# Forming sums of weight blocks once and keeping them in DRAM, in a gated encoder layer on one core

## The chip, the cores and the metric

The kernel runs on one core of one Trainium2 chip. The metric is the device time of one execution in microseconds, and the kernel's time is the median over runs. Every run of a kernel computes the same layer for two sequences of 1024 tokens, the "prompt" and the "sample".

## The reference, cut to what matters

The layer is a gated mix of three token mixers, an output projection with a residual and a layer norm, a SwiGLU feed-forward block, and a second residual and layer norm. All of it is float32. The part that this change touches is the products with `w_gate`, `w_up` and `w_down`:

```python
m = (g[..., :D_MODEL] * ya + g[..., D_MODEL:2 * D_MODEL] * yb + g[..., 2 * D_MODEL:] * yc)
x = layer_norm(DEEPNORM_ALPHA * x + (m @ w_out).astype(x.dtype), ln1_g, ln1_b)
f = (jax.nn.silu(x @ w_gate) * (x @ w_up)) @ w_down        # 1024 -> 2816 -> 1024
x = layer_norm(DEEPNORM_ALPHA * x + f.astype(x.dtype), ln2_g, ln2_b)
```

The same weights serve both sequences.

## The kernel before, in words

**Split products.** Every float32 operand is split into a high half (`wh`, a cast on ScalarE, line 159) and a low half (`wl`, a subtraction on VectorE, line 160), both 128x512 "pages" in a pool of 94 pages. `mm3` (lines 108 to 110) makes one product from three matmuls: high by high, high by low, low by high. A page is 256 KB.

**Quartets.** The products with gate, up and down follow a seven-product scheme for two by two blocks (Strassen's, in Winograd's form). A quartet is four weight blocks B11, B21, B12, B22, each one page. Its seven products use B11, B21, B22 and four sums of blocks: numbers 5 (B12-B11), 6 (B22 minus number 5), 7 (B22-B12) and 4 (B21 minus number 6). `quartet_units` (line 134) lists which raw blocks each product needs; `prepare` (line 162) makes the four sums on GpSimd (line 173, tiles `wt`), 7 us of planned time ahead of the split (`PREP`), and for the first four quartets of a sequence 14 us earlier still (`early`); `split_unit` (line 187) splits whichever page the product needs. One sequence has 22 quartets for gate and up: 11 pairs of column blocks, indexed p = 0 to 10 (`NP` is 11), each with a gate and an up quartet. `w_down` has 11 quartets, used once for both sequences. Two times 22 and 11 make 55 quartets and 220 sums.

**Stages.** For each sequence: the input projections with neighbourhood attention, linear attention and pooling as side work; three gate branches (`gate_branch`, the last one with `w_br_a`); `wout` (16 chunks of 24 matmuls); `gate_up` (154 chunks of 12 matmuls, one product each). After both sequences comes `down`, in five parts of 2, 2, 2, 2 and 3 quartets; each part runs over four token tiles and both sequences, and each such step is seven products of 6 (or 9) matmuls. `gate_up` stores its result in DRAM as split operands, and `down` loads them again (tiles `a`, line 1387).

**Order.** A list of chunks, each with its planned length, is run in order by `run`. Before each chunk, `advance` splits the units that fall due, makes sums `PREP` ahead, and fetches raw pages up to `nraw` (7, and 4 from `down` on) beyond those that are used up. All these loads, and the stores of operands, go out from SyncE's queue, in program order, each waiting there for a free page or for the data that it stores. The `Side` queue holds small steps of other work; chunks call `side.tick`, which runs steps at the rate that `attach` set, and `side.drain` runs what is left. VectorE, ScalarE and GpSimd execute in the program's order too, so a late instruction holds up what stands behind it.

Of the kernel before, what the change touches and what calls it, by code (L numbers as in the profile page):

```python
# [8 lines left out]
F32 = mybir.dt.float32  # L9
# [3 lines left out]
ALU = mybir.AluOpType  # L13
# [64 lines left out]
class Kernel:  # L78
    def __init__(self, tc, ins, xs, ys, pools):
# [12 lines left out]
        self.nraw = NRAW  # L92

# [40 lines left out]
    def quartet_units(self, src, early=0.0):  # L134


        blocks = {}
        for k, j in ((1, 1), (2, 1), (1, 2), (2, 2)):
            ap = src(k, j)
            n, w = ap.shape[1], ap.shape[2]  # L140
            blocks[k, j] = dict(src=[(ap, 0, w)], n=n, w=w)
        q = dict(blocks=blocks, tmp={})
        use = {1: ((1, 1),), 2: ((2, 1),), 6: ((1, 1), (1, 2), (2, 2)), 5: ((1, 1), (1, 2)) if early else (),
               7: ((1, 2), (2, 2)), 4: ((2, 1),), 3: ((2, 2),)}
        return {i: dict(raws=[blocks[x] for x in use[i]], q=q, i=i, early=early if i in (4, 5, 6, 7) else 0.0) for i in use}
# [17 lines left out]
    def prepare(self, u):  # L163
# [12 lines left out]
        if i in (5, 6) and 5 not in tmp:  # L176
            comb(5, B(1, 2), B(1, 1))
        if i == 6:
            comb(6, B(2, 2), tmp[5])
# [67 lines left out]
    def advance(self, upto):  # L247
# [11 lines left out]
        while n < len(order) and order[n]["t"] - order[n].get("early", 0.0) <= upto + PREP:  # L259
            n += 1  # L260
# [758 lines left out]
    def wout(self, S, s):  # L1019
# [198 lines left out]

    def gate_up(self, S, x1_stages, at_end, end_us):
# [5 lines left out]
        for p in range(NP):  # L1225
            for n in ("w_gate", "w_up"):
                src = lambda k, j: self.w_cols(n, (2 * p + j - 1) * 128, 128, 4 * k - 4, 4)
                qs.append(dict(p=p, gate=n == "w_gate", ops=self.quartet_units(src, 14.0 if p < 2 else 0.0)))
# [121 lines left out]
    def down(self, Ss):  # L1350
# [3 lines left out]
        def row(p):  # L1354
            w = self.ins["w_down"][0]
            return lambda k, j: w[(2 * p + k - 1) * 128:(2 * p + k) * 128, (j - 1) * 512:j * 512].rearrange("p (o c) -> p o c", o=1)
# [5 lines left out]
        for part in parts:  # L1362
            ops = [self.quartet_units(row(p)) for p in part]
# [203 lines left out]
    def sequence(self, Ss, s):  # L1567
# [14 lines left out]

        hook(after_cv)
# [8 lines left out]
        def na0():  # L1592
            side.drain()
# [145 lines left out]
```

## Time and profile before

| | us |
|---|---|
| median of 3 runs | 2943.52 (2942.41 to 2944.05) |
| the profiled execution's own time | 2941.66 |
| its span in the trace | 2939.7 |
| TensorE busy | 2850.9 (97%) |
| VectorE busy | 1684.5 (57%) |
| ScalarE busy | 1031.8 (35%) |
| GpSimd busy | 694.5 (24%) |
| granted TensorE clock, mean | 0.988 |

The page gives shares over the whole span, and stages with different limits stand in it side by side. Stages are found in the trace by their tile names: `mh` are the operands of `w_out`, `x1h` those of gate and up, `a` those of down. The `w_out` stage of the first sequence ends at 801 us of the span. 345.06 MB go through the DMA queues in 1410 transfers of SyncE and a few of others.

### The profile page before, as it was taken

To read this page: it belongs to the slowest core of one execution; us is meant where nothing else is said; L and a number is where in the kernel's file an instruction comes from. 1 tells how busy PE (TensorE), PEld (TensorE's weight loads), DVE (VectorE), ACT (ScalarE), POOL (GpSimd) and SP (SyncE) were. 2 spreads that over 40 slices of the span, in tenths; PEclk is the share of its full clock that TensorE was granted. 3 is DMA by queue.
4 is the path that set the end of the run, shared out by engine and by line. 5 is a ranking of instruction groups with operands and counts; after the bars stand their busy time and mean duration, and the time that the engine had idled before them with its cause. 6 is when DMAs were issued, how large, how long until landed. Compare 5 with 4: busy or idle time off the path is not lost.

```text
span 2939.7 us, 39440 instructions
## 1 busy us (share of the span) xinstructions
PE 2850.9 (97%) x14216; PEld 2397.0 (82%) x14216; DVE 1684.5 (57%) x2936; ACT 1031.8 (35%) x2135; POOL 694.5 (24%) x819
## 2 busy tenths in 40 slices
PE   8999999999989999999999999998999999999997
PEld 7888898888767888789888988887788887877876
DVE  5453633433677776673536344347777766567576
ACT  5423322222144444454334122212444444422221
POOL 3221200000222332202202000004133332144367
PEclk9999999999999999999999999999999999999999
DMA  8111111114204655581111111143165554977775
GB/s 223 40 31 44 37 47 43 48 43 133 91 31 136 175 155 158 148 229 51 27 43 47 36 46 46 43 122 108 29 181 161 157 158 149 313 252 255 226 235 198
DMA packets 461346, 345.06 MB, mean 117 GB/s; under 512 B 28257, under 2 KB 395984, under 8 KB 461088
## 3 DMA queue, kind: packets, MB, share of 16 engines
q1 hardware_dynamic: 458800, 337.75, 38.8%
q0 software_dynamic: 2208, 4.74, 0.6%
q8 instruction: 112, 1.84, 0.3%
q14 instruction: 82, 0.67, 0.1%
q10 hardware_dynamic: 144, 0.07, 0.0%
HBM read 242.81 MB, written 102.27 MB: 117 GB/s over the span
## 4 chain that ended last, share of the span: by engine, by line
PE 86%; DVE 8%; ACT 3%; issue 2%; DMA 1%; POOL 1%; SPq 0%; POOLq 0%; DVEq 0%; ACTq 0%
PE ps_m L108 26%; PE ps_m L110 26%; PE ps_m L109 26%; DVE wl L160 3%; PE ps_s L949 1%; PE ps_s L109 1%; PE ps_s L110 1%; PE ps_s L108 1%; DVE x1l L1119 1%; PE ps_s L699 1%; PE ps_s L931 1%; PE ps_s L716 0%; PE ps_s L670 0%; PE ps_s L715 0%; DVE x1s L1132 0%
## 5 line engine op out<-in xcount | busy, mean ns | idle before, releaser
L110 PE MATMUL ps_m<-x1h,wl 128*128 128x512 f32 x1040 | 410.9, 395 | 25.9 <-DVE wl L160 25.8
L108 PE MATMUL ps_m<-xTh,wh 128*128 128x512 f32 x1088 | 435.6, 400 | 0.0
L110 PE MATMUL ps_m<-xTh,wl 128*128 128x512 f32 x1088 | 425.4, 391 | 0.0
L109 PE MATMUL ps_m<-xTl,wh 128*128 128x512 f32 x1088 | 424.8, 390 | 0.0
L108 PE MATMUL ps_m<-x1h,wh 128*128 128x512 f32 x1040 | 409.9, 394 | 3.3 <-ACT wh L159 3.3
L109 PE MATMUL ps_m<-x1l,wh 128*128 128x512 f32 x1040 | 408.9, 393 | 2.1 <-DVE x1l L1119 2.1
L160 DVE TENSOR_TENSOR wl<-raw,wh 128x512 fp32r<-128x512 f32 (+1 forms) x429 | 309.0, 755 | 141.1 <-ACT wh L159 99.5
L173 POOL TENSOR_TENSOR wt<-raw 128x512 f32<-128x512 f32 x110 | 171.2, 1564 | 555.4 <-PE ps_m L109 184.7
L110 PEld LDWEIGHTS ps_m<-x1h,wl 128*128 128x128 f32 x1040 | 197.7, 190 | 72.1 <-DVE wl L160 31.2
L108 PE MATMUL ps_m<-wh,a 128*128 128x512 f32 x616 | 242.6, 394 | 12.0 <-DVE x L1407 4.9
L159 ACT CAST wh<-raw 128x512 fp32r<-128x512 f32 (+1 forms) x429 | 240.1, 604 | 34.4 <-PE ps_m L109 19.7
L109 PE MATMUL ps_m<-wl,a 128*128 128x512 f32 x616 | 241.4, 392 | 0.0
L110 PE MATMUL ps_m<-wh,a 128*128 128x512 f32 x616 | 241.4, 392 | 0.0
L110 PEld LDWEIGHTS ps_m<-xTh,wl 128*128 128x128 f32 x1088 | 204.6, 188 | 43.7 <-DVE wl L160 0.2
L108 PEld LDWEIGHTS ps_m<-xTh,wh 128*128 128x128 f32 x1088 | 205.0, 188 | 41.6 <-issue 1.0
L109 PEld LDWEIGHTS ps_m<-xTl,wh 128*128 128x128 f32 x1088 | 204.9, 188 | 41.0 <-issue 1.0
L108 PEld LDWEIGHTS ps_m<-x1h,wh 128*128 128x128 f32 x1040 | 197.7, 190 | 45.8 <-ACT wh L159 5.2
L109 PEld LDWEIGHTS ps_m<-x1l,wh 128*128 128x128 f32 x1040 | 197.4, 190 | 44.9 <-DVE x1l L1119 4.1
L160 DVE TENSOR_TENSOR wl<-wt,wh 128x512 fp32r<-128x512 f32 x220 | 201.0, 923 | 35.7 <-ACT wh L159 31.6
L999 DVE SCALAR_TENSOR_TENSOR gt<-gt,ps_m 128x512 f32<-128x512 f32 x96 | 65.9, 686 | 270.7 <-PE ps_m L110 263.0
L1216 ACT COPY u<-ps_m 128x512 f32<-128x512 f32 x168 | 98.6, 587 | 320.1 <-PE ps_m L110 302.1
L173 POOL TENSOR_TENSOR wt<-raw,wt 128x512 f32<-128x512 f32 x110 | 170.3, 1554 | 89.0 <-DVE wl L160 27.6
(263 smaller groups left out, 5466.2 us busy)
## 6 DMA issues: line engine op xcount, KB each, us to landing
a<-a SPq DMA_DIRECT2D x264, 256.0 KB, 4.4
raw<-in_w_in SPq DMA_DIRECT2D x168, 256.0 KB, 3.2
a<-wh SPq DMA_DIRECT2D x154, 256.0 KB, 2.9
a<-wl SPq DMA_DIRECT2D x154, 256.0 KB, 3.1
raw<-in_w_gate SPq DMA_DIRECT2D x88, 256.0 KB, 3.6
raw<-in_w_up SPq DMA_DIRECT2D x88, 256.0 KB, 3.9
raw<-in_w_down SPq DMA_DIRECT2D x44, 256.0 KB, 3.8
a<-a SPq DMA_DIRECT2D x88, 128.0 KB, 4.0
```

The costliest lines, as they stand in the source:

```text
L108: mm(out, a[0], b[0], start=start, stop=False, **kw)
L109: mm(out, a[0], b[1], start=False, stop=False, **kw)
L110: mm(out, a[1], b[0], start=False, stop=stop, **kw)
L159: self.nc.scalar.copy(hi, src)
L160: self.side.after.append((of, lambda: self.nc.vector.tensor_tensor(out=lo, in0=src, in1=hi, op=ALU.subtract)))
L173: self.nc.gpsimd.tensor_tensor(out=p, in0=x, in1=y, op=ALU.subtract)
L699: nc.tensor.matmul(bb[:, sl], blk(S.k[h], j)[64:128], blk(S.q[h], j)[64:128], start=True, stop=True)
L931: nc.tensor.transpose(b[0:n, i * 128:i * 128 + 128], s[:, i * 120:i * 120 + n], self.ident)
L949: nc.tensor.matmul(o, v[0:n], p[0:n, i * 128:i * 128 + 128], start=(i == 0), stop=(i == 2))
L999: nc.vector.scalar_tensor_tensor(out=t, in0=t, scalar=1.0, in1=y, op0=ALU.add, op1=ALU.mult)
L1119: self.side.after.append((None, lambda: self.nc.vector.tensor_tensor(out=lo, in0=src, in1=hi, op=ALU.subtract)))
L1216: self.nc.scalar.copy(p, b)
```

## The change

Sums are formed once per quartet and kept in a DRAM tile (`keep`: 128 x 4 x 512, one page per sum). A quartet that is met a second time, or whose sums were made ahead, has seven units with one raw page each, which are loaded as they are and split (`one=True`); GpSimd does nothing for it. A quartet of the first sequence that was not made ahead is summed on GpSimd as before, and `split_unit` adds a store of each sum.

`sum_steps` makes sums ahead, as side steps: load four blocks, two empty steps, four subtractions in place, an empty step, four stores. Items alternate between GpSimd and VectorE. For the first sequence these are ten items: the gate and up quartets of p = 0, 1, 9 and 10, and down's first two quartets; five of them are attached ahead of the last gate branch (over 76 us of planned time) and five at the start of `wout` (over 62 us). For the second sequence they are down's other nine quartets, five and four at the same places. `early` is gone. `nraw` is 4 from the first projections of a sequence to the start of `wout`, where it goes back to 7, and 5 instead of 4 in `down`. The `side.drain()` at the head of `na0` is dropped.

```diff
+    SUMS = (5, 6, 7, 4)
+    def quartet_units(self, key, src):
+        blocks = {x: src(*x) for x in ((1, 1), (2, 1), (1, 2), (2, 2))}
+        n, w = blocks[1, 1].shape[1:]
+        raw = lambda ap: dict(src=[(ap, 0, w)], n=n, w=w)
+        if key in self.kept:
+            d = self.kept[key]
+            whole = {1: blocks[1, 1], 2: blocks[2, 1], 3: blocks[2, 2]}
+            for j, i in enumerate(self.SUMS):
+                whole[i] = d[:, j, :].rearrange("p (a b) -> p a b", a=n)
+            return {i: dict(raws=[raw(whole[i])], one=True) for i in whole}
+        d = self.keep(key)
 ...
+    def sum_steps(self, items):
+        nc = self.nc
+        steps, nop = [], lambda: None
+        for j, (key, src) in enumerate(items):
+            d, B = self.keep(key), {}
+            e = nc.vector if j % 2 else nc.gpsimd
+            def load(B=B, src=src):
+                for x in ((1, 1), (1, 2), (2, 2), (2, 1)):
+                    ap = src(*x)
+                    B[x] = self.page("tb")
+                    nc.sync.dma_start(out=B[x].rearrange("p (a b) -> p a b", a=ap.shape[1]), in_=ap)
+            def sums(out, x, y, B=B, e=e):
+                e.tensor_tensor(out=B[out], in0=B[x], in1=B[y], op=ALU.subtract)
+            def store(B=B, d=d):
+                for j, x in enumerate(((1, 1), (2, 2), (1, 2), (2, 1))):
+                    nc.sync.dma_start(out=d[:, j, :], in_=B.pop(x))
+            steps += [load, nop, nop, lambda f=sums: f((1, 1), (1, 2), (1, 1)), lambda f=sums: f((1, 2), (2, 2), (1, 2)),
+                      lambda f=sums: f((2, 2), (2, 2), (1, 1)), lambda f=sums: f((2, 1), (2, 1), (2, 2)), nop, store]
+        return steps
 ...
     def split_unit(self, u):
             src = q["tmp"][u["i"]]
+            if u["i"] in self.SUMS:
+                self.nc.sync.dma_start(out=q["kept"][:, self.SUMS.index(u["i"]), :], in_=src.rearrange("p a b -> p (a b)"))
             u["op"] = self.split(src, q["blocks"][1, 1]["n"], u)
+            return
+        if "one" in u:
+            r = u["raws"][0]
+            u["op"] = self.split(r.pop("raw"), r["n"], u)
             return
 ...
-        while n < len(order) and order[n]["t"] - order[n].get("early", 0.0) <= upto + PREP:
+        while n < len(order) and order[n]["t"] <= upto + PREP:
 ...
     def wout(self, S, s):
+        self.hook(lambda: setattr(self, "nraw", NRAW))
         self.hook(lambda: self.ln_bcast([S], "ln1"))
+        self.hook(lambda: self.side.attach(S.sums[1], 62.0))
 ...
     def sequence(self, Ss, s):
+        hook(lambda: setattr(self, "nraw", 4))
         hook(after_cv)
 ...
         def na0():
-            side.drain()
             side.attach(nas[0] + (self.more2 if first else []), 52.0)
 ...
+        if first:
+            items = [((n, p), self.gate_src(n, p)) for p in (0, 1, NP - 2, NP - 1) for n in ("w_gate", "w_up")]
+            items += [(("w_down", p), self.down_src(p)) for p in (0, 1)]
+        else:
+            items = [(("w_down", p), self.down_src(p)) for p in range(2, NP)]
+        S.sums = self.sum_steps(items[:5]), self.sum_steps(items[5:])
+        hook(lambda: side.attach(S.sums[0], 76.0))
         self.gate_branch(S, 0, "w_br_a", 4, lambda: S.ya, False, True)
 ...
         if last:
-            hook(lambda: setattr(self, "nraw", 4))
+            hook(lambda: setattr(self, "nraw", 5))
```

The order of the matmuls on TensorE is the same in both programs. Three places where other engines' order moves:

GpSimd where the first sequence goes from `w_out` to gate and up, before. `mv` are layer-norm statistics, two rows for a token tile; the `wt` rows are block sums, and sixteen of them stand behind the last statistics.

```order
L1100 TENSOR_SCALAR mv<-mv 128x1
L1101 TENSOR_TENSOR mv<-mv,mhalf 128x1
L173 TENSOR_TENSOR wt<-raw 128x512 x4
L173 TENSOR_TENSOR wt<-raw,wt 128x512 x4
L173 TENSOR_TENSOR wt<-raw 128x512 x4
L173 TENSOR_TENSOR wt<-raw,wt 128x512 x4
L173 TENSOR_TENSOR wt<-raw 128x512
L173 TENSOR_TENSOR wt<-raw,wt 128x512
```

The same engine in the change, from the end of the last gate branch through the first statistics of `w_out`. `tb` are the blocks of quartets that are summed ahead, `lnb` the norm's weights.

```order
L175 TENSOR_TENSOR tb<-tb 128x512 x12
L1130 DMA lnb<-in_ln_g 128x512 x2
L1130 DMA lnb<-in_ln_b 128x512 x2
L175 TENSOR_TENSOR tb<-tb 128x512 x8
L1144 TENSOR_SCALAR mv<-mv 128x1
L1145 TENSOR_TENSOR mv<-mv,mhalf 128x1
L1144 TENSOR_SCALAR mv<-mv 128x1
L1145 TENSOR_TENSOR mv<-mv,mhalf 128x1
L175 TENSOR_TENSOR tb<-tb 128x512 x4
```

The sixteen sums behind the last statistics are gone in the change, and twenty-four stand ahead of them, the last four among the statistics. Behind these, GpSimd's next sums are those of the fifth quartet.

VectorE in the first half of the first sequence's `w_out`, in the change; before, the two `tb` rows are not there. `acc` is the residual sum, `bst` its statistics.

```order
L1099 SCALAR_TENSOR_TENSOR acc<-acc,ps_m 128x512
L1139 BN_STATS bst<-acc 128x6
L175 TENSOR_TENSOR tb<-tb 128x512 x3
L1099 SCALAR_TENSOR_TENSOR acc<-acc,ps_m 128x512
L1139 BN_STATS bst<-acc 128x6
L175 TENSOR_TENSOR tb<-tb 128x512
```

Four of the stage's eight sums on this engine stand there, among the additions that empty PSUM.

SyncE's queue ahead of `down`'s second part, before. `a` are activations, `res` the residual, `raw` the weight blocks of the second part.

```order
L150 DMA raw<-in_w_down 128x512
L1383 DMA res<-x1e 128x512
L1387 DMA a<-a_75 128x512
L1387 DMA a<-a_76 128x512
L150 DMA raw<-in_w_down 128x512 x3
L1387 DMA a<-a_75 128x512
L1387 DMA a<-a_76 128x512
```

The same place in the change, where `tw_down` are kept sums.

```order
L188 DMA raw<-tw_down_110 128x512
L188 DMA raw<-tw_down_109 128x512
L1434 DMA a<-a_119 128x256
L1434 DMA a<-a_120 128x256
L1390 DMA a_129<-wh 512x1x128
L1390 DMA a_129<-wl 512x1x128
L1434 DMA a<-a_119 128x512
L1434 DMA a<-a_120 128x512
L188 DMA raw<-tw_down_110 128x512
L188 DMA raw<-tw_down_109 128x512
```

Before, eight loads in two groups of four bring a part's blocks; now fourteen come one or two at a time, between the activations' loads.

More of the change, by code (lines that the diff above doesn't have):

```diff
@@ L92, in __init__ @@
         self.nraw = NRAW
+        self.kept = {}
     def page(self, name, dt=F32):
@@ L132, in unit @@
         return dict(raws=raws, per=per, nb=(b + 511) // 512)
[L134 to L145, printed above, removed]
+    SUMS = (5, 6, 7, 4)
@@ new lines, in quartet_units @@
+    def quartet_units(self, key, src):
[9 more added lines that the diff above has]
+        d = self.keep(key)
+        blocks = {x: raw(ap) for x, ap in blocks.items()}
+        q = dict(blocks=blocks, tmp={}, kept=d)
+        use = {1: ((1, 1),), 2: ((2, 1),), 6: ((1, 1), (1, 2), (2, 2)), 5: (), 7: ((1, 2), (2, 2)), 4: ((2, 1),), 3: ((2, 2),)}
+        return {i: dict(raws=[blocks[x] for x in use[i]], q=q, i=i) for i in use}
@@ new lines, in keep @@
+    def keep(self, key):
+        self.kept[key] = self.dram.tile([128, 4, 512], F32, tag="t" + "_".join(map(str, key)), name="t" + "_".join(map(str, key)), bufs=1)
+        return self.kept[key]
+    def sum_steps(self, items):
[17 more added lines that the diff above has]
+        return steps
@@ L175, in comb @@
             return p
-        if i in (5, 6) and 5 not in tmp:
-            comb(5, B(1, 2), B(1, 1))
         if i == 6:
-            comb(6, B(2, 2), tmp[5])
+            comb(6, B(2, 2), comb(5, B(1, 2), B(1, 1)))
         elif i == 7:
@@ L1217, in copy_out, with gate_src, down_src @@
         return p
+    def gate_src(self, n, p):
+        return lambda k, j: self.w_cols(n, (2 * p + j - 1) * 128, 128, 4 * k - 4, 4)
+    def down_src(self, p):
+        w = self.ins["w_down"][0]
+        return lambda k, j: w[(2 * p + k - 1) * 128:(2 * p + k) * 128, (j - 1) * 512:j * 512].rearrange("p (o c) -> p o c", o=1)
     def gate_up(self, S, x1_stages, at_end, end_us):
@@ L1226, in gate_up @@
             for n in ("w_gate", "w_up"):
-                src = lambda k, j: self.w_cols(n, (2 * p + j - 1) * 128, 128, 4 * k - 4, 4)
-                qs.append(dict(p=p, gate=n == "w_gate", ops=self.quartet_units(src, 14.0 if p < 2 else 0.0)))
+                qs.append(dict(p=p, gate=n == "w_gate", ops=self.quartet_units((n, p), self.gate_src(n, p))))
         S.ad = [self.dram.tile([128, 4, 14, 128], F32, tag=f"a{p}", name=f"a{p}") for p in range(NP)]
@@ L1362, in down @@
         for part in parts:
-            ops = [self.quartet_units(row(p)) for p in part]
+            ops = [self.quartet_units(("w_down", p), self.down_src(p)) for p in part]
             for j, i in enumerate(self.USE):
```

3 lines of the change are left out of this document (removed).

## The prediction

> **What bounds the kernel now.** I read the page first: engine shares, the clock, the chain that ended last, the costliest groups.
>
> ```profile
> PE 2850.9 (97%) x14216; PEld 2397.0 (82%) x14216; DVE 1684.5 (57%) x2936; ACT 1031.8 (35%) x2135; POOL 694.5 (24%) x819
> PE 86%; DVE 8%; ACT 3%; issue 2%; DMA 1%; POOL 1%; SPq 0%; POOLq 0%; DVEq 0%; ACTq 0%
> L110 PE MATMUL ps_m<-x1h,wl 128*128 128x512 f32 x1040 | 410.9, 395 | 25.9 <-DVE wl L160 25.8
> L173 POOL TENSOR_TENSOR wt<-raw 128x512 f32<-128x512 f32 x110 | 171.2, 1564 | 555.4 <-PE ps_m L109 184.7
> ```
>
> TensorE (PE) bounds the span; nothing here shortens its work. All that can be won is its idle time (2939.7 - 2850.9 = 88.8 us) and what it loses at a lower clock. The one large wait in a matmul group is in gate and up: 25.8 us for low halves (`wl`) from VectorE (DVE). GpSimd (POOL) makes 220 block sums of about 1.56 us; with a chain share of 1% it looks harmless.
>
> So I asked next for busy time by stretches. The columns are width; PE, weight loads, DVE, ScalarE, GpSimd busy; granted clock; DMA share; GB/s.
>
> ```profile
> 600.00:700.00 100.00, 100.00 (x443) 82.81 (x442) 35.90 (x54) 24.68 (x43) 0.00 (x0) 1.00 0.17 47
> 705.00:770.00 65.00, 65.00 (x289) 53.81 (x288) 28.41 (x46) 8.32 (x16) 3.13 (x6) 1.00 0.32 101
> 770.00:800.00 30.00, 29.36 (x142) 24.07 (x141) 24.29 (x41) 7.33 (x13) 7.65 (x10) 1.00 0.36 126
> 800.00:830.00 30.00, 21.07 (x87) 16.63 (x86) 25.09 (x23) 10.79 (x20) 19.73 (x13) 0.83 0.42 121
> 830.00:900.00 70.00, 63.78 (x272) 49.75 (x271) 52.14 (x72) 34.55 (x62) 12.46 (x9) 0.98 0.11 31
> 1150.00:1250.00 100.00, 94.16 (x434) 76.62 (x433) 62.31 (x83) 43.13 (x80) 24.58 (x16) 0.98 0.52 148
> 2030.00:2060.00 30.00, 21.66 (x98) 17.08 (x96) 26.69 (x25) 11.93 (x21) 19.71 (x13) 0.83 0.45 131
> 2060.00:2150.00 90.00, 84.01 (x360) 66.44 (x359) 66.53 (x91) 42.70 (x79) 18.23 (x12) 0.98 0.19 53
> 2400.00:2500.00 100.00, 93.80 (x396) 75.49 (x395) 67.08 (x84) 40.27 (x75) 36.47 (x24) 0.97 0.49 150
> 2500.00:2600.00 100.00, 100.00 (x443) 82.80 (x442) 55.80 (x77) 35.40 (x63) 20.05 (x15) 1.00 0.96 318
> 2600.00:2850.00 250.00, 238.39 (x1024) 194.42 (x1023) 171.27 (x212) 68.69 (x122) 121.80 (x91) 0.98 0.69 224
> ```
>
> The reader is to see that PE has gaps where GpSimd is busy, and runs through where it is idle (600 to 700: 443 matmuls in 100 us, 0.2257 us each). I count a stretch's loss as idle time plus (1 - clock) x width, an upper estimate, since the clock is also low while PE idles: 800-830 loses 8.9 + 5.1 = 14.0; 830-900 6.2 + 1.4 = 7.6; 1150-1250 5.8 + 2.0 = 7.8; 2030-2060 8.3 + 5.1 = 13.4; 2060-2150 6.0 + 1.8 = 7.8; 2400-2500 6.2 + 3.0 = 9.2; 2600-2850 11.6 + 5.0 = 16.6. Together **76.4 us**, the most that this change can win there.
>
> Why DVE is late shows in the timeline at the first of these places, and in DVE's groups there (804 to 825) and in a stretch where GpSimd rests (550 to 700):
>
> ```profile
> 803.94 2.42 DVE L1076 SCALAR_TENSOR_TENSOR acc<-acc,mv,lnb 128x512 f32<-128x512 f32 x2
> 804.42 6.40 POOL L173 TENSOR_TENSOR wt<-raw 128x512 f32<-128x512 f32 x4
> 806.28 3.41 DVE L1119 TENSOR_TENSOR x1l<-x1f,x1h 128x512 fp32r<-128x512 f32 x2
> 809.62 3.43 DVE L160 TENSOR_TENSOR wl<-raw,wh 128x512 fp32r<-128x512 f32 x2
> 811.41 0.79 PE L110 MATMUL ps_m<-x1h,wl 128*128 128x512 f32 x1 [6.71 <-DVE wl L160]
> 815.85 0.49 PE L108 MATMUL ps_m<-x1h,wh 128*128 128x512 f32 x1
> 819.75 4.05 DVE L160 TENSOR_TENSOR wl<-raw,wh 128x512 fp32r<-128x512 f32 x3
> 821.55 0.50 PE L110 MATMUL ps_m<-x1h,wl 128*128 128x512 f32 x1 [2.22 <-DVE wl L160]
> 823.18 0.63 PE L110 MATMUL ps_m<-x1h,wl 128*128 128x512 f32 x1
> L160 DVE TENSOR_TENSOR wl<-raw,wh 128x512 fp32r<-128x512 f32 x5 | 7.5, 1541 | 0.0
> L160 DVE TENSOR_TENSOR wl<-raw,wh 128x512 fp32r<-128x512 f32 x26 | 16.5, 686 | 3.5 <-PE ps_m L109 2.4 <-issue 1.1
> ```
>
> The same DVE instruction takes 0.686 us alone and 1.541 us while block sums run: a sum costs DVE some 0.86 us. So GpSimd, never named in the wait, makes DVE late, and DVE stops PE.
>
> **The change part by part.** *Sums removed.* Of 220 sums, 56 stay on GpSimd where they were (14 quartets of the first sequence), 44 are made there ahead, 32 ahead on DVE. None is left at the starts and ends of gate and up, or in down.
>
> First start, 800-830: from 803.94 five DVE instructions (two, two, the first `wl`) at 0.69 end at 807.4 instead of 811.41, so the wait of 6.71 becomes 2.7. The next six end at 811.5, ahead of PE, which at full clock needs 5.4 us (24 matmuls x 0.2257) from 807.4: the wait of 2.22 goes. Of the clock's 5.1 I keep 2.2 lost, half of the 4.4 us from 811.41 to 815.85, where matmuls regain their pace, since the clock also fell after the short wait (823.18: 0.63 us). Left 4.9 of 14.0, won 9. The remaining waits of that stage are these (first 826-876, then 876-900):
>
> ```profile
> PE ps_s L109 <- DVE x1l L1119: 2.0, 2, 1.6
> PE ps_s L108 <- ACT x1h L1118: 1.8, 1, 1.8
> PE ps_m L109 <- DVE x1l L1119: 1.1, 1, 1.1
> PE ps_s L109 <- DVE x1l L1119: 0.7, 2, 0.5
> ```
>
> The 2.0 come from DVE's lag and go; with some clock, 3 of 7.6. The rest stays: in the first sequence the fifth quartet's sums still run there. **First start: 12.**
>
> First end, 1150-1250: its sixteen sums are those of the last four quartets, all kept now: **7** of 7.8. Second start: 13.4 - 4.9 = 8.5, and behind it, with no sum left in this sequence, 5.5 of 7.8 (the 1.1, where other DVE work is in the way, and some clock stay): **14**. Second end: 9.2, less some two for a gap with GpSimd idle and its clock: **7**.
>
> ```profile
> 2480.00:2490.00 10.00, 9.26 (x41) 7.35 (x40) 8.72 (x15) 4.87 (x10) 0.00 (x0) 1.00 0.31 101
> ```
>
> Down: its waits come at the part changes, on DVE and ScalarE, which stand behind sums:
>
> ```profile
> PE ps_m L108 <- DVE x L1407: 4.9, 2, 3.0
> PE ps_m L108 <- ACT u L1216: 4.1, 3, 3.2
> PE ps_m L108 <- DVE u L1407: 2.6, 1, 2.6
> 2794.00 0.69 DVE L160 TENSOR_TENSOR wl<-raw,wh 128x512 fp32r<-128x512 f32 x1 [3.21 <-POOL wt L173]
> 2807.10 7.08 DVE L160 TENSOR_TENSOR wl<-wt,wh 128x512 fp32r<-128x512 f32 x3
> ```
>
> Three splits in 7.08 us would take 2.1. But splits of 14 or 21 pages still bunch at a part change, so I take **12** of 16.6. Sum of gains: 12 + 7 + 14 + 7 + 12 = **52**.
>
> *Sums added beside the last gate branch and `w_out`.* The gate branch has room (600-700: DVE 36 of 100, GpSimd 0). `w_out` gets 12 sums on GpSimd and 8 on DVE: 28.4 + 8 x 0.69 + 12 x 0.86 = 44 of 65 us. Hidden by PE, which runs through; with that cover gone, 16 us. The last four fall near the statistics (770-800, DVE 24.3 of 30, PE already short 0.6): between 0 and 4 x 0.86 = 3.4 us in each sequence; I take 1 each, since DVE catches up by 800: **-2**.
>
> *DMA.* The eight quartets of the first sequence go from 4 transfers to 15 (4 loads, 4 stores, 7 loads), the other fourteen from 4 to 8, the second sequence's 22 from 4 to 7, down's eleven from 4 to 15: 88 + 56 + 66 + 121 = 331 more of 256 KB, 345 to 432 MB. All go through SyncE's in-order queue.
>
> ```profile
> SPq L1340 <- ACT wh L159: 231.8, 98, 10.2
> raw<-in_w_gate SPq DMA_DIRECT2D x88, 256.0 KB, 3.6
> 2570.00:2580.00 10.00, 10.00 (x46) 8.29 (x45) 8.09 (x12) 1.77 (x3) 2.90 (x2) 1.00 1.05 383
> ```
>
> In the second gate and up, seven pages ahead are now 7 x 12 x 0.2257 = 19 us (before, at four pages per quartet, 33). A landing takes 3.6, and the longest hold of the queue behind an operand store is 10.2: 14 in 19, hidden by 5. In the first sequence the new stores wait for sums issued 7 us earlier: hidden, with 33 us of reach. With `nraw` 4, the projections still fetch two units of 10.8 us ahead of a landing: hidden. Down is the tight place: activations take 194 GB/s (two quartets of 896 KB per 42 matmuls), fourteen pages in some 23 us another 159: 353, between the 318 that 2500-2600 moved without a gap and the 383 of its best 10 us. The shortfall is at most 35 GB/s x 23 us = 0.8 MB, 2.5 us, at each of five part changes: 0 to 12.5; I take **-3**, since pages are split well before use. The dropped drain moves steps by a few us; I take 0, bounds -3 to 3.
>
> Sum: 52 - 2 - 3 = 47 on the execution of 2941.7, which is 1.9 below the median: 2943.5 - 47 = **2896 us**.
>
> On the clock I go by the row at 823.18: it fell after waits of 6.7 and 2.2 us, so I keep 2.2 lost at each start. The Trainium skill ("TensorE: Matmul & The Clock Gate", Part 1) has it halved only after an idle window of about 3.4 us, free-running. By that rule a lone wait of 2.7 us would mostly leave the clock alone, and the sum would be 51 instead of 47, inside the range.
>
> **The rivals.** *DVE is late by its own work.* For: the gap at 2480-2490 comes with GpSimd idle and DVE at 87%; 770-830 holds DVE at 80% and more. Against: 1.541 against 0.686. Then only the two first waits shrink (9 + 8.5) and half of the ends' gain comes (7), nothing in down: 24.5 - 5 = 20, **2924**.
>
> *Down becomes bound by its loads.* For: 353 GB/s wanted, and loads one by one between activations. Against: DMA share 0.69 over 2600-2850. Price: 2.5 us and the clock's 2.2 at five changes, 23.5 in place of 3: **2917**.
>
> *All 76 go:* 2943.5 - 76.4 = **2867**, if DVE's order leaves no wait at the starts.
>
> *Slower: SyncE's queue.* If it is held over 19 - 3.6 = 15 us, each quartet of the second gate and up shows one landing: 22 x 3.6 = 79 against 47, **2976**. For: every store stands ahead of loads. Against: the longest hold was 10.2. That the change doesn't do what it says is excluded by the order of the instructions.
>
> **How the numbers follow.** Forecast (2880 to 2912) 0.50; DVE's own work 0.15; down's loads 0.12; all gone 0.12; slower 0.05; losses that cancel the gain, 0.06. A measurement of this kernel can tell about 0.2%, 6 us, from no change. Faster 0.50 + 0.15 + 0.12 + 0.12 = 0.89, rounded to 0.88; same 0.06; slower 0.06. The range goes from the full 76 to DVE's own work and the few us that the drain may cost: 2867 to 2926. It leaves out the slower case, the cancelled gain and the tails of the others.
>
> **What would show it.** Right: `wl` near 0.69 us and GpSimd idle at 800-870, PE's first wait there near 2.7 us and in the second sequence too; part changes in down without DVE at 99%; PE unbroken in `w_out`. Wrong: PE waiting for `wh` behind DMA loads in down or in the second gate and up; `wl` still above 1 us where GpSimd rests; a gap ahead of 800.

## The result, and the profile after

| | before | after |
|---|---|---|
| median, us (4 runs each) | 2943.78 (2942.41 to 2944.95) | **2878.70** (2878.20 to 2878.80) |
| ratio, with its 95% interval | | 0.9779 (0.9762 to 0.9796) |
| profiled execution, us (its span) | 2941.66 (2939.7) | 2878.67 (2876.9) |

The change makes the kernel 65 us faster; 47 were forecast. The time lies 1.3 us below the forecast's own band (2880 to 2912) and inside the whole range (2867 to 2926). In the profiled executions the difference is 63.0. First the page of the kernel after: the engines' busy time, the chain that ended last, and the groups that answer to those shown of before.

```profile
PE 2828.9 (98%) x14216; PEld 2388.6 (83%) x14216; DVE 1601.2 (56%) x2968; ACT 1029.9 (36%) x2135; POOL 499.2 (17%) x699
PE 92%; DVE 4%; ACT 2%; issue 1%; DMA 1%; POOL 0%; SPq 0%; POOLq 0%; DVEq 0%; ACTq 0%
L111 PE MATMUL ps_m<-x1h,wl 128*128 128x512 f32 x1040 | 405.9, 390 | 5.0 <-DVE wl L198 5.0
```

GpSimd gave up 195 us of work (694.5 to 499.2). TensorE's idle time in front of the low halves of gate and up went from 25.9 us to 5.0, and the DVE share of the chain from 8% to 4%. TensorE's own busy time fell by 22 us (2850.9 to 2828.9) though it runs the same 14216 matmuls: they ran at a higher clock.

Where the time went is read from busy time by stages. A stage here goes from its first matmul to the first of the next: gate and up of the first sequence, the second sequence up to its gate and up (attention, gates and `w_out`), gate and up of the second, and down. The columns are the stretch, its width, TensorE's busy time with the matmul records in it, granted clock, DMA share, GB/s. Before:

```profile
801.19:1264.02 462.83, 441.84 (x1948) 0.98 0.48 135
1264.02:2032.25 768.23, 764.42 (x4233) 1.00 0.25 70
2032.25:2486.84 454.59, 434.47 (x1883) 0.98 0.48 136
2486.84:2924.89 438.05, 426.03 (x1849) 0.99 0.76 251
```

And after:

```profile
801.68:1242.62 440.94, 434.38 (x1948) 1.00 0.64 189
1242.62:2010.86 768.24, 764.39 (x4234) 1.00 0.33 95
2010.86:2442.12 431.26, 426.11 (x1883) 1.00 0.64 187
2442.12:2862.28 420.16, 419.64 (x1849) 1.00 0.84 278
```

The matmul records in a stage are the same, so widths can be compared. First gate and up won 21.9 us (462.83 - 440.94), the second 23.3, down 17.9: together 63.1, all of the difference. The stage between them, with the sums made ahead beside the last gate branch and `w_out`, took 768.23 and 768.24. Each gain has two parts. Width minus busy time is idle time: 21.0 to 6.6, 20.1 to 5.1 and 12.0 to 0.5, 41 us in all. The busy time itself fell by 7.5, 8.4 and 6.4, 22 us: matmuls that no longer ran at a lowered clock behind a wait. **A third of the gain is the clock.**

The stretches that the prediction added up, in the kernel after (the first end and the second start are taken some 20 us earlier than before, the second end and down 40, since all that lies ahead is shorter; the columns are those of the prediction: width; PE, weight loads, DVE, ScalarE, GpSimd busy; clock; DMA share; GB/s):

```profile
800.00:830.00 30.00, 27.50 (x141) 22.67 (x140) 21.50 (x35) 18.28 (x34) 1.53 (x2) 1.00 0.53 166
830.00:900.00 70.00, 65.93 (x277) 52.35 (x276) 50.47 (x74) 30.73 (x56) 8.26 (x6) 0.98 0.29 85
1128.00:1228.00 100.00, 100.00 (x469) 82.64 (x468) 60.14 (x91) 47.05 (x88) 2.91 (x2) 1.00 0.70 208
2010.00:2040.00 30.00, 27.51 (x134) 22.53 (x133) 20.37 (x32) 16.73 (x31) 1.53 (x2) 0.94 0.49 150
2040.00:2130.00 90.00, 88.09 (x385) 71.61 (x384) 61.33 (x96) 44.94 (x83) 0.00 (x0) 1.00 0.46 132
2360.00:2460.00 100.00, 98.81 (x435) 81.23 (x434) 57.97 (x90) 44.35 (x82) 0.00 (x0) 1.00 0.70 219
2560.00:2810.00 250.00, 249.93 (x1103) 206.60 (x1103) 162.46 (x233) 72.29 (x127) 93.25 (x78) 1.00 0.83 273
```

By the prediction's count (idle time plus what the lower clock takes) they lose 2.5, 5.5, 0, 4.3, 1.9, 1.2 and 0.1: 15.5 us where 76.4 stood. The two longest waits that are left for TensorE in the first gate and up (801.68 to 1242.62):

```profile
PE ps_m L111 <- DVE wl L198: 2.5, 1, 2.5
PE ps_s L109 <- ACT x1h L1162: 2.2, 1, 2.2
```

And the splits at the first start run at their own pace again (DVE's groups, 804 to 825):

```profile
L198 DVE TENSOR_TENSOR wl<-raw,wh 128x512 fp32r<-128x512 f32 x7 | 4.7, 686 | 2.0 <-ACT wh L197 2.0
```

0.686 us, where it took 1.541 before.

### The profile page after: what moved, and what is told of

The parts are those of the page before. It is cut to its first block, busy times and chain, and to the rows that moved or that the text cites. A ratio compares the mean times of both kernels' runs of the same rounds, so it can differ in the third digit from the quotient of the medians.

```text
span 2876.9 us, 39911 instructions
## 1 busy us (share of the span) xinstructions
PE 2828.9 (98%) x14216; PEld 2388.6 (83%) x14216; DVE 1601.2 (56%) x2968; ACT 1029.9 (36%) x2135; POOL 499.2 (17%) x699
## 4 chain that ended last, share of the span: by engine, by line
PE 92%; DVE 4%; ACT 2%; issue 1%; DMA 1%; POOL 0%; SPq 0%; POOLq 0%; DVEq 0%; ACTq 0%
PE ps_m L109 27%; PE ps_m L110 27%; PE ps_m L111 27%; PE ps_s L110 2%; PE ps_s L111 2%; PE ps_s L109 2%; PE ps_s L991 1%; DVE wl L198 1%; PE ps_s L741 1%; PE ps_s L973 1%; PE ps_s L758 0%; PE ps_s L712 0%; PE ps_s L757 0%; PE ps_s L1154 0%; DVE qs L655 0%
## 5 line engine op out<-in xcount | busy, mean ns | idle before, releaser
L198 DVE TENSOR_TENSOR wl<-raw,wh 128x512 fp32r<-128x512 f32 (+1 forms) x593 | 410.1, 722 | 148.3 <-ACT wh L197 139.4
L197 ACT CAST wh<-raw 128x512 fp32r<-128x512 f32 (+1 forms) x593 | 336.6, 608 | 75.4 <-DVE wl L198 30.5
L1454 POOL TENSOR_TENSOR u<-u,u 128x512 f32<-128x512 f32 x62 | 83.8, 1352 | 680.0 <-DVE u L1456 545.2
L109 PE MATMUL ps_m<-wh,xTh 128*128 128x256 f32 (+1 forms) x640 | 186.2, 291 | 4.4 <-ACT wh L197 4.4
L110 PE MATMUL ps_m<-wl,xTh 128*128 128x256 f32 (+1 forms) x640 | 184.0, 287 | 0.7 <-DVE wl L198 0.5
```

The lines of the kernel that those rows point to most:

```text
L109: mm(out, a[0], b[0], start=start, stop=False, **kw)
L110: mm(out, a[0], b[1], start=False, stop=False, **kw)
L197: self.nc.scalar.copy(hi, src)
L198: self.side.after.append((of, lambda: self.nc.vector.tensor_tensor(out=lo, in0=src, in1=hi, op=ALU.subtract)))
L1454: (e or nc.vector).tensor_tensor(out=a, in0=a, in1=b, op=ALU.add)
```

## The experiments

The leading theory is the prediction's: each block sum on GpSimd stretches VectorE's work, and VectorE then stops TensorE. Rivals: the sums simply came late; part of the gain is the change's other edits; transfers in down nearly eat the gain. Stage widths below come from the same view as above, one profiled execution each; medians and ratios from the timed runs, each against runs of before on the same chip.

| run | median, us | ratio (95%) | gate and up 1 | gate and up 2 | down |
|---|---|---|---|---|---|
| before | 2943.8 | | 462.8 | 454.6 | 438.1 |
| after | 2878.7 | 0.9779 (0.9762 to 0.9796) | 440.9 | 431.3 | 420.2 |
| gate and up's sums alone | 2895.8 | 0.9845 (0.9830 to 0.9861) | 440.6 | 431.3 | 439.4 |
| down's sums alone | 2924.4 | 0.9941 (0.9922 to 0.9960) | 463.9 | 454.0 | 420.3 |
| subtractions nobody reads | 2908.9 | 0.9891 (0.9874 to 0.9908) | 453.4 | 441.2 | 432.5 |
| the same, of two pages | 2925.7 | 0.9943 (0.9928 to 0.9958) | 455.0 | 445.2 | 436.8 |
| the same, and waited for | 2929.5 | 0.9962 (0.9948 to 0.9977) | 456.6 | 446.8 | 436.0 |
| memsets nobody reads | 2890.3 | 0.9826 (0.9811 to 0.9842) | 446.3 | 431.4 | 428.3 |
| before, sums on VectorE | 2910.9 | 0.9893 (0.9876 to 0.9909) | 452.8 | 437.7 | 435.0 |
| side edits undone | 2877.2 | 0.9778 (0.9764 to 0.9793) | 440.6 | 431.3 | 419.8 |
| down's pages loaded twice | 3068.2 | 1.0427 (1.0411 to 1.0442) | 442.5 | 431.3 | 609.6 |
| the same, into other pages | 2904.0 | 0.9873 (0.9857 to 0.9889) | 442.4 | 431.2 | 446.3 |
| fifth quartet ahead too | 2877.9 | 0.9783 (0.9768 to 0.9799) | 440.6 | 431.2 | 420.4 |
| and the seventh norm later | **2870.2** | 0.9760 (0.9744 to 0.9776) | 436.6 | 427.2 | 419.8 |

### Do the halves add up?

First the change without its part for down: down's quartets are summed on GpSimd again, with four raw pages ahead.

```diff
-        d = self.keep(key)
+        d = None if key[0] == "w_down" else self.keep(key)
...
-            items += [(("w_down", p), self.down_src(p)) for p in (0, 1)]
...
-            items = [(("w_down", p), self.down_src(p)) for p in range(2, NP)]
+            items = []
```

> The change without its down part: down's eleven quartets are summed on GpSimd as before, nothing of w_down is made ahead, nraw in down is 4 again. Theory (block sums on GpSimd slow VectorE while they run, stage by stage): gate and up keep their gain (441 and 431 us instead of 463 and 455), down goes back from 420 to about 438 us; the whole some 18 us over the change, 2897. Rival (the gain comes from loads, queue and pages as a whole): down keeps part of its gain, since gate and up leave the queue and the pages alone differently; under 2888.

Then down's part alone: gate and up's quartets are summed on GpSimd in both sequences, 14 us early for the first four, as before.

```diff
-        d = self.keep(key)
+        early = 14.0 if key[1] < 2 else 0.0
...
-            items = [((n, p), self.gate_src(n, p)) for p in (0, 1, NP - 2, NP - 1) for n in ("w_gate", "w_up")]
-            items += [(("w_down", p), self.down_src(p)) for p in (0, 1)]
+            items = [(("w_down", p), self.down_src(p)) for p in (0, 1)]
```

> The change for down alone: gate and up of both sequences are summed on GpSimd as before, the first quartets 14 us early, nothing of them is stored. Theory: down takes 420 us instead of 438, gate and up stay at 463 and 455; the whole 2944 - 18 = 2926. Together with the run without down's part the two gains add up to the whole 65. Rival: the gains do not add up.

Measured 2895.8 and 2924.4. Each half changes its own stages (the others stay within 1.3 us of before), and each of its stages has the width of the full change (440.6, 431.3; 420.3). By the stages the gains add: 22.2, 23.3 and 17.8 us, where the whole change won 63.1. By the medians they are 44.6 and 16.0 of 65. No stage paid for another.

### Is it the interference, or that sums came late?

Five runs bear on it. In the first four, GpSimd is given work again at the places where it made sums before (for the first four quartets of a sequence 14 us early, as there), while the kept sums stay in use.

First, a subtraction of the loaded page from itself wherever a kept sum is loaded (164 of them), into a page that nobody reads:

```diff
+            early = 14.0 if key[0] != "w_down" and key[1] < 2 else 0.0
...
+            elif "one" in u:
+                self.fetch(u["need"])
+                if u["i"] in self.SUMS:
+                    self.idle_sum(u["raws"][0])
...
+    def idle_sum(self, r):
+        out = self.scr[:, 0:r["n"] * r["w"]].rearrange("p (a b) -> p a b", a=r["n"])
+        self.nc.gpsimd.tensor_tensor(out=out, in0=r["raw"], in1=r["raw"], op=ALU.subtract)
```

> The change with 164 subtractions on GpSimd put back where block sums stood: for each kept sum one tensor_tensor on the page just loaded, of the same shape, into a scratch page that nobody reads. Nothing waits for them. Theory (contention with VectorE): most of the 63 us come back, 2925 to 2945, with VectorE's splits at 1.4 to 1.7 us and waits of 5 us and more at the starts of gate and up. Rival (TensorE waited because the sums themselves came late, or because of the loads): within 5 us of 2879.

2908.9, between the two expectations. The splits and the wait at the first start are as the theory had them (1.383 and 5.8 us), but only 34.6 us of the three stages' 63.1 came back (12.4, 9.9 and 12.3 in the table). These subtractions are shorter than before's sums, 1.23 us on average. So the next run subtracts a second page, of zeros:

```diff
-        self.nc.gpsimd.tensor_tensor(out=out, in0=r["raw"], in1=r["raw"], op=ALU.subtract)
+        self.nc.gpsimd.tensor_tensor(out=v(self.scr), in0=r["raw"], in1=v(self.scr0), op=ALU.subtract)
```

> The change, with a subtraction of two different pages on GpSimd wherever a kept sum is now loaded (164 of them, each reading the loaded page and a page of zeros, writing a page nobody reads). As with the subtraction of a page from itself, nobody waits for it. If the missing half of the loss is that those subtractions were shorter than before's sums (1.23 us against 1.56): at 1.56 us a piece the loss goes up by at least a quarter, 2916 or more, and up to 2941 if it explains all. If the missing half is that somebody waited for the sums: 2905 to 2912 again.

2925.7: 14.1, 13.9 and 16.7 came back, 44.7 of 63.1, and in down nearly all. Groups of GpSimd over the whole span in the run with the shorter subtractions:

```profile
L325 POOL TENSOR_TENSOR scr<-raw 128x512 f32<-128x512 f32 x164 | 201.7, 1230 | 461.8 <-DMA raw<-tw_gate 235.5 <-DMA raw<-tw_up 125.0 <-DMA raw<-tw_down 95.8
```

In the run with two pages, over the span, and then DVE's at the first start, 804 to 825:

```profile
L325 POOL TENSOR_TENSOR scr<-raw,scr 128x512 f32<-128x512 f32 x164 | 245.2, 1495 | 434.8 <-DMA raw<-tw_gate 223.9 <-DMA raw<-tw_up 116.0 <-DMA raw<-tw_down 88.0
L199 DVE TENSOR_TENSOR wl<-raw,wh 128x512 fp32r<-128x512 f32 x5 | 8.5, 1754 | 0.0
```

And TensorE's first wait in gate and up, from its timeline:

```profile
812.72 0.80 PE L111 MATMUL ps_m<-x1h,wl 128*128 128x512 f32 x1 [6.66 <-DVE wl L199]
```

22% more GpSimd time (201.7 to 245.2) brought 29% more loss by the stages of the profiled executions (34.6 to 44.7), and more than that by the medians (30 to 47). Nothing reads these results, and yet the wait is back at 6.66 us (6.71 before) and `wl` at 1.75 us; in down, 9.5 of TensorE's 10.7 us of waits are for VectorE. **That GpSimd's work slows VectorE and so stops TensorE is shown.** Work that nobody waits for brings back some 70% of what the change won; how much of that could be something else, the memsets below bound.

For the rest, each subtraction then wrote a page of its own, and the splits read that page, so that they wait for GpSimd as before:

```diff
+        u["sum"] = v(self.page("wt"))
...
-            u["op"] = self.split(r.pop("raw"), r["n"], u)
+            x = r.pop("raw")
+            u["op"] = self.split(u.pop("sum", x), r["n"], u)
```

> The run with subtractions of two pages on GpSimd, with one thing more: each subtraction (the loaded sum less a page of zeros, so its value stays the sum) goes to a page of its own, and the splits read that page and so wait for GpSimd, as they did for before's sums. That run without the wait stood at 2925.7, 46 of the 63 us back. If the 17 us that it leaves are splits waiting for the sums: 2938 to 2946, the time of before. If the waiting costs nothing by itself and they come from elsewhere (four pages loaded for a quartet at once, the order of the sums): within 4 us of 2926.

2929.5 (2925.1 to 2931.6, against 2922.9 to 2928.4 without the wait): between the two expectations, nearer the second. The medians put the price of waiting at 4 us, with ranges and intervals that overlap, so that it may be nothing. In the trace it shows at the first end, in TensorE's waits from 1150 on. Before:

```profile
PE ps_m L110 <- DVE wl L160: 4.9, 3, 1.9
PE ps_m L108 <- ACT wh L159: 1.0, 1, 1.0
```

Without and with the wait for the subtractions:

```profile
PE ps_m L109 <- ACT wh L198: 0.7, 1, 0.7
```

```profile
PE ps_m L111 <- DVE wl L199: 1.9, 3, 1.1
PE ps_m L109 <- ACT wh L198: 1.7, 2, 1.0
```

5.9 us before, 0.7 without the wait, 3.6 with it. What is left of the difference to before, 10 us against the runs of before on the same chip (2939.4 - 2929.5; by the ratio's interval 7 to 15) and by the stages nearly all in gate and up, **stays open**. What no run here put back is that product 6 needs two sums in a row and three raw pages at once, and that a quartet loads four raw pages instead of seven. That the first quartets' sums come 14 us early is not the cause: these runs have it too.

The fourth run gives GpSimd work that only writes: a copy of one column, then three memsets of a page, at the same 164 places.

```diff
-        self.nc.gpsimd.tensor_tensor(out=out, in0=r["raw"], in1=r["raw"], op=ALU.subtract)
+        self.nc.gpsimd.tensor_copy(self.scr[:, 0:1], r["raw"][:, 0, 0:1])
+        for _ in range(3):
+            self.nc.gpsimd.memset(self.scr, 0.0)
```

> As the run with subtractions put back, but GpSimd writes only: for each kept sum one copy of a single column of the loaded page (so that it comes at the same time) and three memsets of a scratch page, about as long together as a sum (0.33 us for 256 columns in the profile of before, so some 0.6 each). If any work of GpSimd slows VectorE: as with the subtractions, 2925 or more. If only GpSimd's reading does: within 6 us of 2879, with splits near 0.7 us while memsets run. The Trainium skill (SBUF - State Buffer, Who interferes with whom) says the second: a VectorE instruction with two SBUF inputs contends with a GpSimd instruction that reads SBUF, not with one that only writes it.

2890.3, outside both expectations, but its stages tell them apart. Groups of GpSimd over the span, and of DVE at the first start:

```profile
L326 POOL MEMSET scr<- 128x512 f32 x492 | 259.4, 527 | 28.6
L199 DVE TENSOR_TENSOR wl<-raw,wh 128x512 fp32r<-128x512 f32 x7 | 4.7, 686 | 3.6 <-ACT wh L198 3.6
```

GpSimd is busier than with subtractions (259.4 us in memsets alone), and the splits keep their 0.686 us; the second gate and up has the width of the change (431.4). Over that whole stage the 161 splits of weight pages take 0.687 us on average beside memsets, and 0.838 beside the subtractions of two pages. The Trainium skill ("SBUF — State Buffer", Who interferes with whom) says the same: a VectorE instruction with two inputs in SBUF contends with a GpSimd instruction that reads SBUF, not with one that only writes. By that rule the run should have cost nothing but GpSimd's queue. It lost 5.4, 0.1 and 8.1 us in the three stages. In the 5.4 no queue shows: the wait of 2.50 us at the first start is as long as in the change but lowered the clock this time (0.57 over 808 to 812), and one more wait, 2.08 us, stands behind splits that real sums stretch, those of a quartet that is still summed on GpSimd there:

```profile
960.45 1.78 DVE L199 TENSOR_TENSOR wl<-as,wh 128x512 fp32r<-128x512 f32 x1
963.95 0.50 PE L111 MATMUL ps_m<-x1h,wl 128*128 128x512 f32 x1 [2.08 <-DVE wl L199]
```

The 8.1 are the queue. GpSimd's timeline, with ScalarE and TensorE, in down:

```profile
2765.76 1.70 POOL L326 MEMSET scr<- 128x512 f32 x3
2769.43 3.71 POOL L1464 TENSOR_TENSOR u<-u,u 128x512 f32<-128x512 f32 x3
2771.94 1.66 ACT L198 CAST wh<-raw 128x512 fp32r<-128x512 f32 x3 [8.14 <-POOL u L1464]
2772.61 0.80 PE L109 MATMUL ps_m<-wh,a 128*128 128x512 f32 x1 [5.36 <-ACT wh L198]
```

Real work of GpSimd (`u`) stands behind a row of memsets, ScalarE waits 8.14 us for it, and TensorE 5.36 for ScalarE. This one place makes most of the 8.1 us that down lost. If all 13.6 us of this run are taken off the 44.7 of the two-page subtractions, 31 us are left, half of what the change won: an estimate, on the low side, of what the interference alone costs.

Last, the kernel before with its sums made in place by VectorE itself:

```diff
-            self.nc.gpsimd.tensor_tensor(out=p, in0=x, in1=y, op=ALU.subtract)
+            self.nc.vector.tensor_tensor(out=p, in0=x, in1=y, op=ALU.subtract)
```

> The kernel before, with its block sums at the same places made by VectorE instead of GpSimd; nothing kept in DRAM. The theory that the loss of before is VectorE held up by GpSimd's sums: a sum then costs VectorE its own 0.69 us, where beside GpSimd each cost it some 0.86 us of stretched operations; so most of the loss stays and the time is 2920 to 2935. The rival, that the matrix unit waited because sums on GpSimd (1.56 us each, in a queue) came late: the sums come in 0.69 us, and 2880 to 2905.

2910.9, between the two expectations: about half of the loss is gone. The 220 sums show in DVE's groups:

```profile
L173 DVE TENSOR_TENSOR wt<-raw,wt 128x512 f32<-128x512 f32 x110 | 75.1, 687 | 2.3 <-DMA raw<-in_w_down 0.3 <-DMA raw<-in_w_up 0.2
L173 DVE TENSOR_TENSOR wt<-raw 128x512 f32<-128x512 f32 x110 | 74.3, 684 | 5.8 <-DMA raw<-in_w_up 5.5 <-DMA raw<-in_w_gate 0.3
```

A sum costs VectorE 0.69 us on its own queue. The first gate and up got back 10.0 of 21.9 us, the second 16.9 of 23.3 (454.6 to 437.7), down only 3.0 of 17.9. A part change there, by busy time (columns as in the prediction):

```profile
2608.00:2616.00 8.00, 5.29 (x24) 4.04 (x22) 7.93 (x12) 3.68 (x8) 1.67 (x1) 0.96 0.91 296
```

VectorE is full (7.93 of 8) and TensorE short of 2.7 us. The single instruction on GpSimd, a `u` of down, stretches one split by 1 us (two of them take 2.38); the rest of VectorE's twelve run at their own pace, so here it is mostly the amount of its work that makes it late. This run changes the wait, the queue and the interference at once, so it doesn't split the loss further.

### What do the transfers and the side edits cost?

The three small edits (four raw pages ahead in down instead of five, no lowering to four from the projections on, the drain back in its place) undone together:

```diff
-        hook(lambda: setattr(self, "nraw", 4))
...
+            side.drain()
...
-            hook(lambda: setattr(self, "nraw", 5))
+            hook(lambda: setattr(self, "nraw", 4))
```

> The change as it is, with its three side edits undone: the raw pages loaded ahead stay four in the down product and are not set back ahead of gate and up, and the drain of the side work stands where it stood. The theory that the whole gain is the sums taken off GpSimd: within 3 us of 2879. The rival that part of the gain is one more page loaded ahead in the down product: at least 8 us above 2879, all of them in the down stage.

2877.2 and a down stage of 419.8: they do nothing that can be measured.

To find the margin of down's loads, every page of its quartets was loaded twice:

```diff
-        for src, c0, n in r["src"]:
+        for src, c0, n in r["src"] * r.get("times", 1):
```

> The change, with every page of the down product's kept quartets loaded twice into the same place (77 pages, some 20 MB more, in the 420 us of the down stage). The prediction's price of transfers in the down product (353 GB/s wanted at the change of a part, up to 8 us for each change that is fed too slowly) gives with the pages doubled at least 2900, the loss in the down stage alone. The rival, that the loads had a wide margin there and the 3 us for transfers were nothing: the stage stays within 4 us of 420 and the time under 2884.

3068.2, the stage at 609.6: far beyond both expectations, and not for the bytes. SyncE's and TensorE's waits in down:

```profile
SPq L188 <- DMA raw<-tw_down: 134.8, 39, 6.9
SPq L188 <- DMA raw<-in_w_down: 93.2, 29, 4.9
PE ps_m L109 <- DMA a<-a: 119.7, 28, 9.9
```

The second load of a page into the same place waits for the first to land, in SyncE's in-order queue, 228 us in all, and the activations (`a`) behind it come late. So the run measured that wait. Loaded into three other pages in turn instead, it comes nearer to the bytes:

```diff
+        if r.get("extra"):
+            self.scr.append(self.scr.pop(0))
+            self.nc.sync.dma_start(out=self.scr[0].rearrange("p (a b) -> p a b", a=r["n"]), in_=r["src"][0][0])
```

> The change, with every page of the down product's kept quartets loaded once more, ahead of it, into one of three pages that nobody reads (77 pages, 20 MB more). Here the second load waits for no first one, as it did when both went to the same page. If the 189 us of that run were bytes: again a down stage above 500 us. If they were the wait of the queue for the first landing: under 450 us; and if the loads had the wide margin that the missing 3 us speak of, the stage stays within 5 us of 420 and the time within 6 us of 2879. The prediction's price for transfers (up to 8 us for each change of a part that is fed too slowly, five changes) gives 440 to 460 for the stage.

2904.0, the stage 446.3 us, 26 more, inside the expected 440 to 460. The 8 us a change of the two expectations are not the prediction's own figure, though, which was 2.5 us and 2.2 of clock. Counted its way, doubled pages want 194 + 2 x 159 = 512 GB/s for 23 us, against 318 to 383: an estimated 8 to 14 us at each change, 39 to 70 in all. The measured price is below that. Nor need all 26 be bytes: in down SyncE's queue waits 30.5 us in all for landings of weight pages, against 14.5 in the kernel after. TensorE's waits in down in this run:

```profile
PE ps_m L109 <- DMA a<-a: 18.8, 12, 4.4
```

One stretch around a part change (columns as in the prediction):

```profile
2592.00:2642.00 50.00, 45.78 (x198) 36.58 (x198) 31.70 (x43) 12.59 (x22) 12.27 (x9) 1.00 1.03 367
```

The same stretch of the kernel after:

```profile
2592.00:2642.00 50.00, 50.00 (x222) 41.41 (x221) 31.90 (x44) 12.74 (x23) 14.51 (x11) 1.00 0.97 334
```

The mechanism that the prediction named exists: at a part change the DMA engines reach a share of 1.03 at 367 GB/s and TensorE waits for `a`. The change as it is moves 334 GB/s there and waits for no load. The rate alone doesn't decide it, though: at the part change before, both kernels move 351 GB/s, and only this run (first) has gaps, the kernel after (second) none:

```profile
2492.00:2542.00 50.00, 45.58 (x197) 36.09 (x196) 25.62 (x39) 17.79 (x32) 3.92 (x3) 1.00 1.02 351
2492.00:2542.00 50.00, 50.00 (x222) 41.38 (x222) 28.48 (x43) 18.28 (x33) 5.49 (x4) 1.00 1.02 351
```

The 20 MB would take 55 us at 367 GB/s; they cost 26, so about half of them still found room. Down had a margin that the prediction did not count on, and the price comes only beyond it.

### What was left to win?

The 2.2 us wait at 881 in the first sequence stands behind the fifth quartet's sums. So p = 2 was made ahead too, beside the last gate branch:

```diff
-            items = [((n, p), self.gate_src(n, p)) for p in (0, 1, NP - 2, NP - 1) for n in ("w_gate", "w_up")]
+            items = [((n, p), self.gate_src(n, p)) for p in (0, 1, 2, NP - 2, NP - 1) for n in ("w_gate", "w_up")]
...
-        hook(lambda: side.attach(S.sums[0], 76.0))
+        hook(lambda: side.attach(S.sums[0], 82.0 if first else 76.0))
```

> The change, with the fifth gate and up quartet of the first sequence (p = 2, both matrices) made beside the last gate branch too, so that its sums are off GpSimd at the start of gate and up. The theory that the 2.25 us wait of the first start (x1h, behind those sums) is the last loss that the sums leave: 3 to 5 us less, about 2875. The rival, that the two more items slow the last gate branch or move the same wait to the next quartet: 2878 to 2884.

2877.9, no difference that can be told, as the rival had it. In the timeline of the kernel after, and of this one, at the next quartets that are still summed on GpSimd:

```profile
881.16 0.50 PE L109 MATMUL ps_s<-x1h,wh 128*128 128x512 f32 x1 [2.25 <-ACT x1h L1162]
```

```profile
952.68 1.30 POOL L211 TENSOR_TENSOR wt<-raw 128x512 f32<-128x512 f32 x1 [6.89 <-DVE as L1358]
954.45 1.78 DVE L198 TENSOR_TENSOR wl<-as,wh 128x512 fp32r<-128x512 f32 x1
957.95 0.50 PE L111 MATMUL ps_m<-x1h,wl 128*128 128x512 f32 x1 [2.22 <-DVE wl L198]
```

The wait moved: the next sums stretch a split to 1.78 us, and TensorE waits 2.22 us at 958, where it waited for nothing before.

On top of it, the seventh row tile's normalization was moved behind the first product of gate and up, in both sequences:

```diff
-                    if ch == 1 and t:
+                    if ch == 1 and 0 < t < 7:
                         norm(t - 1)
...
-                        S.late = [lambda: norm(7), lambda: spill(6), lambda: spill(7)]
+                        S.late = [lambda: norm(6), lambda: norm(7), lambda: spill(6), lambda: spill(7)]
...
-                    self.side.attach([S.late.pop(0)] + [nop] * 6 + x1_stages[0] + [nop], 92 * MM512)
+                    self.side.attach([S.late.pop(0), nop, S.late.pop(0)] + [nop] * 4 + x1_stages[0] + [nop], 92 * MM512)
```

> The run with the fifth quartet ahead, and in both sequences the normalization of the seventh row tile moved from the end of w_out behind the first product of gate and up, beside that of the eighth, so that VectorE has some 3 us less ahead of the first product's low parts. The 2.5 us wait of each start is VectorE's own queue (busy all of the 8 us before it): it shrinks by 2 us or more in both, 4 to 8 us less than the run with the fifth quartet alone, 2867 to 2871. The rival, that the row tile then comes late for the transposes behind it (the waits move there): within 2 us of that run.

**2870.2** (2868.9 to 2874.7, against 2876.4 to 2879.7 on the same chip): as expected, and ahead of both kernels. The two gate and up stages of the last run and of this one:

```profile
799.55:1240.10 440.55, 433.92 (x1947) 1.00 0.64 188
2008.30:2439.55 431.25, 426.04 (x1884) 1.00 0.64 187
```

```profile
800.63:1237.19 436.56, 432.34 (x1948) 1.00 0.64 189
2005.39:2432.64 427.25, 424.46 (x1884) 1.00 0.64 188
```

Each stage is 4.0 us shorter: 2.4 of idle time (6.6 to 4.2; 5.2 to 2.8), and 1.6 of busy time. The wait of 2.5 us is gone from both starts, and with it the clock that it cost (in the last run 0.57 over the 4 us behind each).

## Why the prediction was right, and where it was short

The direction and the mechanism held; the sum of 47 was 16 us short, 9 of them in down. By its number, the rival "all 76 go" (2867) lies nearer to 2878.7 than the forecast (2896); by its condition, that no wait is left at the starts, it did not come.

**First start and end, 12 + 7 = 19; measured 21.9.** The steps held in detail: the first wait was to become 2.7 us and is 2.50, the one of 2.22 behind it is gone, `wl` is back at 0.69 us. Sums left on GpSimd keep one wait (2.25 us at 881), as the prediction said they would. The end lost nothing any more, instead of 0.8.

**Second start and end, 14 + 7 = 21; measured 23.3.** The wait at the start is 2.49 us, as in the first sequence. At the end, 1.2 us are left where two and their clock were to stay.

**The clock, 2.2 us kept lost at each start.** The pair of runs with the norm moved, where the clock had fallen behind both waits, puts the price of one at 1.6 us. It isn't paid each time. In the kernel after the same wait left the clock at 1.00 in the first start and not in the second (stretches of 4 us behind the two waits: width, TensorE busy, clock):

```profile
808.00:812.00 4.00, 4.00 (x19) 1.00 0.56 158
2018.00:2022.00 4.00, 4.00 (x12) 0.57 0.57 158
```

In the first sequence it fell behind the wait of 2.25 us at 881 instead (0.57 over 881.2 to 885.2). So the stretch from 800 to 830 lost 2.5 us where 4.9 were to stay, and 830 to 900 lost 5.5 where 4.6 were. The two errors cancel in part, and that is luck: the prediction had no way to tell which wait would pay.

The Trainium skill ("TensorE: Matmul & The Clock Gate", Part 1) has the clock halved after a free-running idle window of about 3.4 us. That equal waits end differently fits a free-running window; that 2.5 us were enough doesn't fit its length, and the measurement decides. By the rule the sum would have been 51, nearer to what was measured, though what was missing lay in down.

**Down, 12 - 3 = 9; measured 17.9.** This is the step that failed, in two terms. "Splits of 14 or 21 pages still bunch at a part change" kept 4.6 of 16.6 us lost; in fact 0.1 is left in that stretch, and TensorE waits 0.5 us in the whole stage. VectorE's own work at the part changes fits once no sums stretch it, though only just: the sign "without DVE at 99%" did not come, as VectorE is busy 9.79 and 9.90 of 10 us at two changes (2590 to 2600, 2665 to 2675), with TensorE at 10.00 in both. And transfers were given 3 us for a shortfall of 0.8 MB at each change. The shortfall came from taking 318 GB/s as what moves without a gap; the kernel after moves 351 over 50 us without one, its trace shows no wait for a load, and the run with 20 MB more shows that such waits do come beyond it.

**Sums beside the last gate branch and `w_out`, -2; measured 0.** The second sequence's stage took 768.23 us before and 768.24 after, with nine of down's quartets summed beside it. The first sequence's part is 0.5 us longer in the profile, which is less than two runs with the same program up to there differ (801.7 in the kernel after, 800.0 in the run with down's pages loaded twice). No gap opened ahead of 800: TensorE is busy 65.00 of the 65 us from 705 and 29.36 of the 30 from 770, as before.

**The rivals.** "DVE's own work" (2924) falls with down, which lost no time to it, and with the starts, whose left waits are as long as forecast; it does own the 2.5 us at each start, as moving the norm showed. "Down's loads" (2917) didn't come, but 20 MB more bring waits of its kind. "All 76 go" (2867): by the prediction's count 15.5 us were left, and moving a norm took 8 off the time. "SyncE's queue" (2976) didn't come; the run with each page loaded twice shows what a held queue does, in down (3068).

**One link was too short.** The prediction priced a sum at 0.86 us of VectorE and took lateness from that alone. Work that nobody waits for brings back 70% of the gain (at least half by interference alone, by the estimate above), with the waiting perhaps some points more; about 10 us of before have a cause that no run isolated.

## What to carry to other kernels

An engine that no wait names can still set the time: look for instructions of a bound engine's feeder that take twice their own duration, and see what runs beside them. Work on GpSimd that reads SBUF is paid for by VectorE's two-input work; work that can be done once, or earlier beside a stage with room, is worth its extra transfers as long as the loads still land in time (here down ran free at a mean of 278 GB/s, and 20 MB more made TensorE wait for loads). Count a wait of TensorE with the clock behind it: here a third of the gain was clock.

## What the runs showed of the hardware that was not expected

- GpSimd work that only writes leaves VectorE alone: at the first start memsets of 0.53 us stand beside splits of 0.686 us, where subtractions of two pages make the same splits 1.75 us long.
- A subtraction of a page from itself takes GpSimd 1.23 us on average, of two pages 1.50, and the loss grew with it (34.6 to 44.7 us).
- A TensorE wait of 2.5 us lowered the clock in one of two places of the same execution, to 0.57 over the next 4 us. In another run it lowered it in both; there, taking the wait away was worth 4.0 us each.
- A load into a page whose last load has not landed holds SyncE's queue until it has: 68 such waits, 228 us, for 20 MB that cost 26 us when they went elsewhere.
